# One decoder layer on one core: the second key block's attention product taken in one matmul, stages of the projection phase placed anew, and the first norm's vectors loaded through SyncE's queue

## The chip, the cores and the metric

The kernel runs on one core of one Trainium2 chip. The metric is the device time of one execution in microseconds (us). TensorE is written PE, its weight loads PEld, VectorE DVE, ScalarE ACT, GpSimd POOL and SyncE SP; SP only issues transfers and waits.

## The reference, cut to what matters

```python
proj  = x @ W_in                      # q | k | v | B | C | h | gate_attn | gate_conv
y_att = attention(q, k, v) @ W_att    # 8 heads of 64, partial rotary, causal
y_cnv = (B * causal_dwconv3(C * h)) @ W_cnv
mix   = (sigmoid(g_att) * y_att + sigmoid(g_cnv) * y_cnv) @ W_o
x     = LayerNorm(alpha * x + mix)
u     = causal_dwconv3(x @ W_up);  f = (silu(u_gate) * u_val) @ W_down
x     = LayerNorm(alpha * x + f)
```

There are 256 positions and a model width of 1024, all in float32. The block length of the attention is 256, so that with 256 positions each query attends to its own block alone: ordinary causal attention over two 128-position halves. The second half of the keys is seen by the second half of the queries only.

## The kernel before

**Products.** Every float32 product is made of three TensorE products of rounded parts: a factor is split into a high part (an ACT copy that rounds) and a low part (the DVE difference of the source and the high part), and `mm3` (lines 329 to 331) multiplies high by high, high by low and low by high. Weights come in 1 MB chunks from a packed tensor on SP's queue (line 187) into `raw`, are split on ACT (`wh`, line 211) and DVE (`wl`, line 221) half a chunk (a unit) at a time, and are used once. There are 3 `raw` buffers and 9 of `wh` and of `wl`.

**Order.** The order of all engines is written by hand. After q, k and v, PE works through numbered slots, one unit of weights and 12 matmuls of 512 columns in most: slots 0 to 11 make h, C and B, 12 to 27 the four gate blocks, 28 to 35 the two mixers' output products (`y`, in the order first and second 128 positions of the first 512 columns, then of the second 512; even slots multiply the convolution's `yT`, odd ones the attention's `aT`), 36 to 43 the product with W_o (`o`). The function `slot` first issues a slot's products, then the ACT and DVE work placed at that slot. The table `STEPS` gives each stage of the attention, the convolution and the gates a step: step 2u lies before and 2u + 1 behind the splits of slot u, and keys that end in E choose the engine (1 is DVE) of a copy. `lah` and `lal` say how many units ahead the splits run in each slot. Stages of PE (`s`, the scores, and `av`, the attention's second product) are placed by whole slots, behind the slot's own products.

**Attention.** It runs by pairs p = 0 to 3 of heads. `masked`, `exps` and `normalize` make a pair's probabilities; their 16-bit halves are turned by a transposing transfer (SP, line 476), joined again (`probs_words`), and split into high and low part in `PT` (`probs_h` on ACT, line 487; `probs_l` on DVE). `PT` is a single buffer, so that the next pair's `probs_h` waits for the matmuls of `attend`. The weights of those matmuls hold v's high and low part side by side, so one product gives both, 64 partitions each. `attend_out` copies the lower 64 partitions, `attend_sum` adds them to the upper 64, and `attend_h` and `attend_l` split the sum into `aT`.

**PSUM.** 4 banks take the accumulators of the projections; 4 more (`ps_bank`) take the scores and then the attention's products, and from slot 28 on the pairs of banks of `y`.

**Mix and first norm.** For each of the four pieces of `y` DVE makes the gated sum (`mix_conv`, `mix_att`), its 16-bit halves (`mix_halves`) are turned by a transfer on SP's queue (line 859; the third piece in two halves of 256 columns), joined (`mix_words`, lines 865 and 867) and split into `mT` (`mix_h`, line 874, and `mix_l`), which W_o's product reads. The joining and the splitting of a piece stand one behind the other: both halves of the third piece are joined before either is split. Then come the residual sum and the first norm (lines 908 to 926), PE's transposes of the first 128 positions (`x1t`, line 976) and the feed-forward part, which the change does not reach but for one store near the end.

The norm's two vectors are spread over all partitions by two transfers of 512 KB (line 902), issued by POOL into a buffer that `aT` held before:

```python
    ln1 = big.tile([P, 2, D], F32, tag="d8", name="ln1")
    for i, g in enumerate((ln1_g, ln1_b)):
        nc.gpsimd.dma_start(ln1[:, i, :], bass.AP(tensor=g.tensor, offset=g.offset, ap=[[0, P], [1, D]]))
```

Of the kernel before, what the change touches and what calls it, by code (L numbers as in the profile page):

```python
# [13 lines left out]
AF = mybir.ActivationFunctionType  # L14
ALU = mybir.AluOpType

P = 128
S = 256
# [125 lines left out]
def layer_kernel(ctx: ExitStack, tc: tile.TileContext, x, wpack, cpack, b_gate, ln1_g, ln1_b, ln2_g, ln2_b, out):  # L144
# [32 lines left out]
    def issue_dma(c):  # L177
        nonlocal xr
        while len(raws) <= c and len(raws) < len(chunks):
# [8 lines left out]
            if i == XR_CHUNK:  # L188
                xr = big.tile([P, 2, D], F32, tag="x", name="xr")
                for row in range(2):  # L190
                    nc.sync.dma_start(xr[:, row], x[0, row * P:(row + 1) * P])
# [300 lines left out]
    def attend(p):  # L492


        o = PR[p, "o"] = ps_bank(f"av{p}").rearrange("p (j s) -> p j s", j=2)
        for j in range(2):
            js = slice(j * P, (j + 1) * P)
            for a in range(2):
                nc.tensor.matmul(o[:, j], vp[:, 0, p, js], PT[:, a, j, 0:256], start=a == 0, stop=False)
            for a in range(2):  # L500
                nc.tensor.matmul(o[:, j, P:S], vp[:, 1, p, js], PT[:, a, j, 256:384], start=False, stop=a == 1)

    def attend_out(p):

        c = PR[p, "c"] = scratch([P, 2, S], f"ac{p}")
        nc.scalar.activation(c[0:HD], PR[p, "o"][HD:P], AF.Copy)

    def attend_sum(p):
        c, o = PR[p, "c"], PR[p, "o"]
        nc.vector.tensor_tensor(c[HD:P, 0], o[0:HD, 1], c[0:HD, 1], op=ALU.add)  # L510
        nc.vector.tensor_tensor(c[0:HD, 0], o[0:HD, 0], c[0:HD, 0], op=ALU.add)
# [66 lines left out]
    STEPS = {'vl': [2, 0], 'qw': [5, 6, 9, 11], 'qwE': [0, 1, 1, 0], 'qh': [7, 9, 10, 15], 'ql': [6, 8, 14, 15], 's': [5, 10], 'ml': [6, 7, 10, 10], 'm': [15, 18, 21, 27], 'e': [17, 20, 26, 32], 'n': [19, 23, 32, 38], 'w': [22, 25, 37, 43], 'wE': [0, 1, 0, 0], 'h': [23, 27, 40, 44], 'l': [24, 32, 42, 45], 'av': [13, 18, 22, 24], 'out': [27, 42, 45, 51], 'sum': [40, 43, 50, 50], 'ah': [42, 44, 52, 52], 'al': [45, 48, 52, 55], 'c1': [21, 32], 'c2a': [23, 24, 38, 39], 'c2d': [24, 29, 44, 41], 'c3': [33, 48], 'c4a': [35, 51], 'c4d': [43, 53], 'sig': 17, 'hc': [6, 8], 'zm': [15, 15], 'zh': [17, 15], 'zhE': [0, 1], 'bh': [27, 26], 'bj': [32, 33], 'bjE': [0, 1], 'c1E': [0, 0], 'lah': [5, 6, 7, 5, 5, 5, 5, 5, 4, 3, 4, 4, 4, 4, 3, 5, 5, 5, 5, 4, 4, 3, 5, 6, 7, 6, 5, 6, 6, 6, 7, 6, 6, 6, 6, 4, 2, 4, 3, 6, 7, 8, 8, 8], 'lal': [2, 5, 4, 4, 3, 3, 4, 5, 3, 3, 3, 3, 4, 3, 2, 4, 4, 4, 4, 3, 2, 2, 2, 3, 6, 6, 4, 3, 5, 5, 5, 5, 5, 5, 5, 3, 3, 4, 3, 4, 6, 6, 5, 6], 'sg': [35, 35, 46, 48, 50, 53, 61, 61], 'gb': [23, 34, 43, 50], 'gs': [31, 32, 41, 38, 48, 48, 59, 57], 'yc': [59, 63, 67, 70], 'ya': [61, 65, 69, 71], 'yaE': [0, 1, 0, 0], 'yh': [64, 66, 71, 71], 'yhE': [0, 0, 0, 1], 'yw': [68, 70, 75, 85], 'ywE': [0, 1, 0, 0], 'mh': [68, 72, 75, 85], 'mlo': [69, 73, 78, 84], 'mlw': [11, 15, 21, 22]}  # L578
# [322 lines left out]
    for i, g in enumerate((ln1_g, ln1_b)):  # L901
        nc.gpsimd.dma_start(ln1[:, i, :], bass.AP(tensor=g.tensor, offset=g.offset, ap=[[0, P], [1, D]]))
# [373 lines left out]
    for c in range(2):  # L1276
        cc = slice(c * 512, (c + 1) * 512)
        norm_apply(r0[:, cc], r0[:, cc], mv, ln2[:, 0, cc], ln2[:, 1, cc])
        for a in range(0, P, P // 2):
            nc.sync.dma_start(out[0, a:a + P // 2, cc], r0[a:a + P // 2, cc])  # L1280
# [75 lines left out]
```

## Time and profile before

| | |
|---|---|
| three timed runs | 352.75, 358.1 and 358.31 us; median 358.1 |
| profiled execution, its own time | 354.5 us |
| its span, first to last instruction | 352.4 us |
| mean granted TensorE clock in it | 0.995 |
| PE busy in the span | 344.6 us, 98% |
| DVE, ACT, POOL busy | 295.5, 253.2, 16.0 us |
| moved | 81.64 MB, 232 GB/s in the mean |

A matmul's busy time overlaps that of the next, since matmuls are pipelined; how fast PE works is read from the distance of starts. In the timeline a row has start, duration, engine, line, operation, the names of output and inputs, the shape and the count, and in brackets the idle time before it with what ended it.

### The profile page before, as it was taken

How to read it: one execution, taken by the hardware profiler on the slowest of the kernel's cores; microseconds unless marked ns; L12 is line 12 of the kernel's file. 1: busy time of each engine (PE TensorE's matmuls, PEld its weight loads, DVE VectorE, ACT ScalarE, POOL GpSimd, SP SyncE). 2: the span in 40 equal slices, each digit the busy share in tenths (PEclk: the TensorE clock that was granted, in tenths of full speed). 3: DMA queues.
4: the chain of work that ended last, by engine and by line, in shares of the span. 5: the costliest groups of instructions: out<-in, count | busy, mean ns of one | idle time of the engine just before them, and what ended most of it. 6: DMA issues, size and time to landing. Idle time of an engine off the chain costs nothing.

```text
span 352.4 us, 4621 instructions
## 1 busy us (share of the span) xinstructions
PE 344.6 (98%) x1595; PEld 286.1 (81%) x1595; DVE 295.5 (84%) x504; ACT 253.2 (72%) x386; POOL 16.0 (5%) x38
## 2 busy tenths in 40 slices
PE   9999999999999999999999999999999999999993
PEld 8888888888888888778888888888888888888883
DVE  4787769699999988799945999899799969597975
ACT  4766957799889855495566879879487878677800
POOL 2000002010000000104100000000000000000030
PEclk9999999999999999999999999999999999999998
DMA  7995968669956999985499668686887958667003
GB/s 275 426 378 223 215 188 333 95 204 272 274 170 223 340 368 218 269 293 200 74 286 313 248 163 248 218 268 184 328 227 295 307 173 267 171 262 151 0 18 102
DMA packets 56151, 81.64 MB, mean 232 GB/s; under 512 B 45632, under 2 KB 46144, under 8 KB 49088
## 3 DMA queue, kind: packets, MB, share of 16 engines
q1 hardware_dynamic: 55552, 79.25, 73.1%
q0 software_dynamic: 576, 2.10, 1.9%
q8 instruction: 12, 0.20, 0.2%
q14 instruction: 11, 0.09, 0.1%
HBM read 69.28 MB, written 1.05 MB: 200 GB/s over the span
## 4 chain that ended last, share of the span: by engine, by line
PE 86%; DVE 5%; DMA 4%; issue 2%; ACT 1%; POOL 0%; POOLq 0%; DVEq 0%; ACTq 0%
PE u L331 10%; PE u L329 10%; PE u L330 10%; PE qk L644 6%; PE d L331 5%; PE d L330 5%; PE d L329 5%; PE g L329 4%; PE g L330 4%; PE g L331 4%; DMA mixw<-mixw 4%; PE u L1117 3%; PE v L644 3%; DVE wl L221 1%; PE b L329 1%
## 5 line engine op out<-in xcount | busy, mean ns | idle before, releaser
L221 DVE TENSOR_TENSOR wl<-raw,wh 128x1024 fp32r<-128x1024 f32 x100 | 119.4, 1220 | 14.6 <-ACT wh L211 14.3
L211 ACT ACTIVATE wh<-raw 128x1024 fp32r<-128x1024 f32 x97 | 98.5, 1053 | 7.6 <-DMA raw<-in_wpack 4.5
L329 PE MATMUL u<-wh,x1T 128*128 128x512 f32 x160 | 62.3, 390 | 0.0
L331 PE MATMUL u<-wh,x1T 128*128 128x512 f32 x160 | 62.3, 389 | 0.0
L330 PE MATMUL u<-wl,x1T 128*128 128x512 f32 x160 | 62.3, 389 | 0.0
L330 PEld LDWEIGHTS u<-wl,x1T 128*128 128x128 f32 x160 | 30.0, 188 | 6.3
L331 PEld LDWEIGHTS u<-wh,x1T 128*128 128x128 f32 x160 | 30.0, 188 | 6.3
L329 PEld LDWEIGHTS u<-wh,x1T 128*128 128x128 f32 x160 | 30.0, 188 | 6.2
L244 DVE TENSOR_TENSOR wl<-raw,wh 128x1024 fp32r<-128x1024 f32 (+2 forms) x27 | 24.8, 955 | 7.7 <-ACT wh L243 7.5
L998 ACT ACTIVATE fc<-pb,consts 128x256 f32<-128x256 f32 x44 | 19.9, 500 | 15.5 <-DVE pb L1044 15.5
L331 PE MATMUL d<-wh,f 128*128 128x512 f32 x76 | 29.6, 390 | 0.0
L329 PE MATMUL d<-wh,f 128*128 128x512 f32 x76 | 29.6, 390 | 0.0
L330 PE MATMUL d<-wl,f 128*128 128x512 f32 x76 | 29.6, 389 | 0.0
L1032 ACT ACTIVATE up<-u 128x1024 uint16<-128x1024 uint16 x22 | 21.3, 1013 | 7.2 <-PE u L331 7.1
L243 ACT ACTIVATE wh<-raw 128x1024 fp32r<-128x1024 f32 (+2 forms) x27 | 21.3, 834 | 7.2 <-DMA raw<-in_wpack 7.2
L329 PE MATMUL g<-wh,xT 128*128 128x512 f32 x64 | 25.2, 393 | 0.0
L330 PE MATMUL g<-wl,xT 128*128 128x512 f32 x64 | 25.0, 390 | 0.0
L331 PE MATMUL g<-wh,xT 128*128 128x512 f32 x64 | 24.9, 389 | 0.0
L1006 DVE SCALAR_TENSOR_TENSOR fc<-pb,consts,fc 128x254 f32<-128x254 f32 x44 | 21.3, 484 | 1.6
L1004 DVE SCALAR_TENSOR_TENSOR fc<-pb,consts,fc 128x255 f32<-128x255 f32 x44 | 21.1, 480 | 0.0
L644 PE MATMUL qk<-wh,xT 128*128 128x512 f32 x60 | 19.2, 390 | 0.0
L330 PEld LDWEIGHTS d<-wl,f 128*128 128x128 f32 x76 | 14.3, 188 | 3.0
(221 smaller groups left out, 644.3 us busy)
## 6 DMA issues: line engine op xcount, KB each, us to landing
raw<-in_wpack SPq DMA_DIRECT2D x55, 1024.0 KB, 5.3
raw<-in_wpack SPq DMA_DIRECT2D x6, 896.0 KB, 11.5
gb<-in_b_gate SPq DMA_DIRECT2D x4, 256.0 KB, 5.2
xr<-in_x SPq DMA_DIRECT2D x2, 512.0 KB, 7.0
ln<-in_ln_g POOLq DMA_DIRECT2D x2, 512.0 KB, 5.1
ln<-in_ln_b POOLq DMA_DIRECT2D x2, 512.0 KB, 5.8
raw<-in_wpack SPq DMA_DIRECT2D x2, 384.0 KB, 4.4
raw<-in_wpack SPq DMA_DIRECT2D x2, 256.0 KB, 3.0
```

Of the source, the lines that this page charges most:

```text
L211: nc.scalar.activation(units[u]["h"], raw_of(u), AF.Copy)
L221: (eng or nc.vector).tensor_tensor(units[u]["l"], raw_of(u), units[u]["h"].bitcast(F32), op=ALU.subtract)
L243: nc.scalar.activation(h, src, AF.Copy)
L244: (eng or nc.vector).tensor_tensor(l, src, h.bitcast(F32), op=ALU.subtract)
L329: nc.tensor.matmul(o, ah, bh, start=start, stop=False)
L330: nc.tensor.matmul(o, ah, bl, start=False, stop=False)
L331: nc.tensor.matmul(o, al, bh, start=False, stop=stop)
L644: nc.tensor.matmul(banks[m][t], (xl if p == 2 else xh)[:, k, t * P:(t + 1) * P], wl if p == 1 else wh, start=k == 0 and p == 0, stop=k == ...
L998: nc.scalar.activation(PB["c", i][a], PB[i][:, a * S:(a + 1) * S], AF.Copy, scale=w_ffn(2, j))
L1004: nc.vector.scalar_tensor_tensor(c[:, 1:S], pb[:, a * S:a * S + S - 1], w_ffn(1, j), c[:, 1:S], op0=ALU.mult, op1=ALU.add)
L1006: nc.vector.scalar_tensor_tensor(c[:, 2:S], pb[:, a * S:a * S + S - 2], w_ffn(0, j), c[:, 2:S], op0=ALU.mult, op1=ALU.add)
L1032: nc.scalar.activation(half.rearrange("p (w n) -> p w n", w=2), PB["rows", c][t].bitcast(U16).rearrange("p (n w) -> p w n", w=2), AF.Copy)
```

## The change

1. `attend`: the two products of the second key block with the probabilities' high and low part, 128 columns each and added in one place, become one product of 256 columns into two places. Each half j of a pair gets a bank of its own, 384 columns of it used. `attend_out` becomes two copies of 256 columns, `attend_sum` gets two more sums, of 128 columns, that add the low part's place.
2. `STEPS` has other numbers in 144 of its 253 places: stages and split distances move by a few half slots, and four copies change their engine.
3. The first norm's two vectors are issued by SP in place of POOL, at the same place of the program. `xr` comes in one transfer of 1 MB in place of two, and the first half of the first output rows leaves in one store in place of two.

```diff
@@ issue_dma @@
-                for row in range(2):
-                    nc.sync.dma_start(xr[:, row], x[0, row * P:(row + 1) * P])
+                nc.sync.dma_start(xr, x[0].rearrange("(t p) d -> p t d", p=P))
@@ attend @@
-        o = PR[p, "o"] = ps_bank(f"av{p}").rearrange("p (j s) -> p j s", j=2)
+        PR[p, "o"] = []
         for j in range(2):
+            o = ps_bank(f"av{p}{j}")
+            PR[p, "o"].append(o)
             js = slice(j * P, (j + 1) * P)
             for a in range(2):
-                nc.tensor.matmul(o[:, j], vp[:, 0, p, js], PT[:, a, j, 0:256], start=a == 0, stop=False)
-            for a in range(2):
-                nc.tensor.matmul(o[:, j, P:S], vp[:, 1, p, js], PT[:, a, j, 256:384], start=False, stop=a == 1)
+                nc.tensor.matmul(o[:, 0:S], vp[:, 0, p, js], PT[:, a, j, 0:256], start=a == 0, stop=a == 1)
+            nc.tensor.matmul(o[:, P:P + S].rearrange("p (a n) -> p a n", a=2), vp[:, 1, p, js], PT[:, :, j, 256:384],
+                             start=False, stop=True, skip_group_check=True)
@@ attend_out @@
-        nc.scalar.activation(c[0:HD], PR[p, "o"][HD:P], AF.Copy)
+        for j in range(2):
+            nc.scalar.activation(c[0:HD, j], PR[p, "o"][j][HD:P, 0:S], AF.Copy)
@@ attend_sum @@
-        nc.vector.tensor_tensor(c[HD:P, 0], o[0:HD, 1], c[0:HD, 1], op=ALU.add)
-        nc.vector.tensor_tensor(c[0:HD, 0], o[0:HD, 0], c[0:HD, 0], op=ALU.add)
+        for j in range(2):
+            nc.vector.tensor_tensor(c[0:HD, j, P:S], o[j][0:HD, S:S + P], c[0:HD, j, P:S], op=ALU.add)
+        nc.vector.tensor_tensor(c[HD:P, 0], o[1][0:HD, 0:S], c[0:HD, 1], op=ALU.add)
+        nc.vector.tensor_tensor(c[0:HD, 0], o[0][0:HD, 0:S], c[0:HD, 0], op=ALU.add)
@@ the first norm's vectors @@
-        nc.gpsimd.dma_start(ln1[:, i, :], bass.AP(tensor=g.tensor, offset=g.offset, ap=[[0, P], [1, D]]))
+        nc.sync.dma_start(ln1[:, i, :], bass.AP(tensor=g.tensor, offset=g.offset, ap=[[0, P], [1, D]]))
@@ the last norm of the first rows @@
-        for a in range(0, P, P // 2):
-            nc.sync.dma_start(out[0, a:a + P // 2, cc], r0[a:a + P // 2, cc])
+        rows = P // (c + 1)
+        for a in range(0, P, rows):
+            nc.sync.dma_start(out[0, a:a + rows, cc], r0[a:a + rows, cc])
```

Of the table, the keys that matter below, by pair of heads (or by piece of the mix):

| key | stage | before | now |
|---|---|---|---|
| `av` | attention's second product (slot) | 13, 18, 22, 24 | 14, 19, 22, 23 |
| `al` | low part of `aT` | 45, 48, 52, 55 | 45, 47, 55, 55 |
| `c4d` | low part of `yT` | 43, 53 | 39, 54 |
| `qwE` | engine that joins the turned q and k | 0, 1, 1, 0 | 0, 1, 0, 0 |
| `zhE`, `bjE` | engines of two copies of the convolution | 0, 1 and 0, 1 | 1, 1 and 0, 0 |
| `yh`, `yhE` | halves of the mix | 64, 66, 71, 71; 0, 0, 0, 1 | 64, 66, 71, 74; 0, 0, 0, 0 |
| `yw` | joining of the turned mix | 68, 70, 75, 85 | 67, 71, 77, 86 |

On PE, at the third pair's attention product behind slot 22 (`av` is its bank, `vpt` holds v and `PT`, `g` is a gate block), before:

```order
L331 MATMUL g_1057<-wh_999,xT 128x512
L499 MATMUL av_1117<-vpt 128x256 x2
L501 MATMUL av_1117<-vpt 128x128 x2
L499 MATMUL av_1117<-vpt 128x256 x2
L501 MATMUL av_1117<-vpt 128x128 x2
L329 MATMUL g_1056<-wh_1028,xT 128x512
```

and now:

```order
L330 MATMUL g_1063<-wh_980,xT 128x512
L500 MATMUL av_1123<-vpt 128x256 x2
L501 MATMUL av_1123<-vpt 128x256
L500 MATMUL av_1127<-vpt 128x256 x2
L501 MATMUL av_1127<-vpt 128x256
L328 MATMUL g_1062<-wh_994,xT 128x512
```

Eight matmuls have become six, into two banks; the place is the same. The first two pairs' products stand one slot later than before, the fourth pair's one slot earlier, 12 matmuls behind the third's.

On SP, at the mix (`mixw` holds the halves, `raw` weights), before:

```order
L859 DMA_TRANSPOSE mixw<-mixw 128x8x128
L187 DMA raw_1420<-in_wpack 128x2048
L859 DMA_TRANSPOSE mixw<-mixw 128x4x128 x2
L859 DMA_TRANSPOSE mixw<-mixw 128x8x128
L187 DMA raw_1508<-in_wpack 128x2048
```

and now:

```order
L863 DMA_TRANSPOSE mixw<-mixw 128x8x128
L187 DMA raw_1405<-in_wpack 128x2048
L863 DMA_TRANSPOSE mixw<-mixw 128x4x128 x2
L906 DMA ln_1462<-in_ln_g 128x1024
L906 DMA ln_1462<-in_ln_b 128x1024
L863 DMA_TRANSPOSE mixw<-mixw 128x8x128
L187 DMA raw_1490<-in_wpack 128x2048
```

The norm's vectors stand behind the two transposes of the third piece and ahead of that of the fourth, whose halves ACT now writes and not DVE.

On DVE, ahead of the first `y` products (`ac` is the attention's sum, `ct` the convolution's result), before:

```order
L510 TENSOR_TENSOR ac_1224<-av_1181,ac_1224 64x256
L511 TENSOR_TENSOR ac_1224<-av_1181,ac_1224 64x256
L221 TENSOR_TENSOR wl_1231<-raw_1130,wh_1195 128x1024
L240 TENSOR_TENSOR aT<-ac_1136,aT 128x256
L240 TENSOR_TENSOR yT<-ct_1045,yT 128x2x256
L240 TENSOR_TENSOR aT<-ac_1224,aT 128x256
L221 TENSOR_TENSOR wl_1295<-raw_1157,wh_1267 128x1024
L221 TENSOR_TENSOR wl_1297<-raw_1157,wh_1269 128x1024
```

and now:

```order
L513 TENSOR_TENSOR ac_1227<-av_1156,ac_1227 64x128
L513 TENSOR_TENSOR ac_1227<-av_1160,ac_1227 64x128
L514 TENSOR_TENSOR ac_1227<-av_1160,ac_1227 64x256
L515 TENSOR_TENSOR ac_1227<-av_1156,ac_1227 64x256
L220 TENSOR_TENSOR wl_1261<-raw_1134,wh_1198 128x1024
L239 TENSOR_TENSOR yT<-ct_1014,yT 128x2x256
L220 TENSOR_TENSOR wl_1281<-raw_1166,wh_1237 128x1024
L220 TENSOR_TENSOR wl_1283<-raw_1166,wh_1259 128x1024
L239 TENSOR_TENSOR aT<-ac_1189,aT 128x256
L239 TENSOR_TENSOR aT<-ac_1227,aT 128x256
```

Both low parts of `aT` stand behind two more weight splits than the first of them did, and each pair's sums are four in place of two.

More of the change, by code (lines that the diff above doesn't have):

```diff
@@ L577, in layer_kernel @@
     C0 = U[OFF_H]
-    STEPS = {'vl': [2, 0], 'qw': [5, 6, 9, 11], 'qwE': [0, 1, 1, 0], 'qh': [7, 9, 10, 15], 'ql': [6, 8, 14, 15], 's': [5, 10], 'ml': [6, 7, 10, 10], 'm': [15, 18, 21, 27], 'e': [17, 20, 26, 32], 'n': [19, 23, 32, 38], 'w': [22, 25, 37, 43], 'wE': [0, 1, 0, 0], 'h': [23, 27, 40, 44], 'l': [24, 32, 42, 45], 'av': [13, 18, 22, 24], 'out': [27, 42, 45, 51], 'sum': [40, 43, 50, 50], 'ah': [42, 44, 52, 52], 'al': [45, 48, 52, 55], 'c1': [21, 32], 'c2a': [23, 24, 38, 39], 'c2d': [24, 29, 44, 41], 'c3': [33, 48], 'c4a': [35, 51], 'c4d': [43, 53], 'sig': 17, 'hc': [6, 8], 'zm': [15, 15], 'zh': [17, 15], 'zhE': [0, 1], 'bh': [27, 26], 'bj': [32, 33], 'bjE': [0, 1], 'c1E': [0, 0], 'lah': [5, 6, 7, 5, 5, 5, 5, 5, 4, 3, 4, 4, 4, 4, 3, 5, 5, 5, 5, 4, 4, 3, 5, 6, 7, 6, 5, 6, 6, 6, 7, 6, 6, 6, 6, 4, 2, 4, 3, 6, 7, 8, 8, 8], 'lal': [2, 5, 4, 4, 3, 3, 4, 5, 3, 3, 3, 3, 4, 3, 2, 4, 4, 4, 4, 3, 2, 2, 2, 3, 6, 6, 4, 3, 5, 5, 5, 5, 5, 5, 5, 3, 3, 4, 3, 4, 6, 6, 5, 6], 'sg': [35, 35, 46, 48, 50, 53, 61, 61], 'gb': [23, 34, 43, 50], 'gs': [31, 32, 41, 38, 48, 48, 59, 57], 'yc': [59, 63, 67, 70], 'ya': [61, 65, 69, 71], 'yaE': [0, 1, 0, 0], 'yh': [64, 66, 71, 71], 'yhE': [0, 0, 0, 1], 'yw': [68, 70, 75, 85], 'ywE': [0, 1, 0, 0], 'mh': [68, 72, 75, 85], 'mlo': [69, 73, 78, 84], 'mlw': [11, 15, 21, 22]}
@@ new lines, in layer_kernel @@
+    STEPS = {'vl': [0, 3], 'qw': [5, 6, 8, 10], 'qwE': [0, 1, 0, 0], 'qh': [5, 9, 8, 15], 'ql': [5, 9, 14, 16], 's': [5, 10], 'ml': [6, 7, 10, 10], 'm': [15, 18, 22, 25], 'e': [18, 20, 26, 31], 'n': [18, 22, 31, 39], 'w': [22, 26, 39, 43], 'wE': [0, 1, 0, 0], 'h': [24, 29, 40, 44], 'l': [24, 30, 42, 45], 'av': [14, 19, 22, 23], 'out': [28, 39, 48, 50], 'sum': [37, 40, 49, 50], 'ah': [43, 46, 52, 52], 'al': [45, 47, 55, 55], 'c1': [23, 31], 'c2a': [24, 25, 37, 38], 'c2d': [24, 27, 43, 43], 'c3': [36, 48], 'c4a': [38, 51], 'c4d': [39, 54], 'sig': 17, 'hc': [8, 8], 'zm': [16, 17], 'zh': [17, 18], 'zhE': [1, 1], 'bh': [27, 24], 'bj': [35, 38], 'bjE': [0, 0], 'c1E': [0, 0], 'lah': [4, 6, 7, 6, 5, 5, 4, 5, 5, 4, 6, 5, 6, 6, 6, 6, 6, 6, 5, 4, 5, 3, 5, 5, 7, 7, 7, 7, 5, 6, 7, 6, 6, 7, 7, 4, 4, 5, 2, 5, 5, 4, 5, 6], 'lal': [3, 6, 4, 4, 3, 4, 4, 4, 3, 4, 5, 4, 5, 4, 5, 5, 4, 4, 4, 3, 2, 2, 2, 3, 6, 5, 5, 6, 5, 5, 5, 5, 4, 6, 6, 3, 3, 5, 3, 3, 3, 2, 2, 2], 'sg': [36, 36, 46, 50, 51, 54, 67, 64], 'gb': [25, 37, 44, 50], 'gs': [31, 31, 41, 42, 48, 48, 58, 58], 'yc': [60, 63, 68, 70], 'ya': [62, 65, 69, 72], 'yaE': [0, 0, 0, 0], 'yh': [64, 66, 71, 74], 'yhE': [0, 0, 0, 0], 'yw': [67, 71, 77, 86], 'ywE': [0, 1, 0, 0], 'mh': [67, 73, 77, 87], 'mlo': [69, 74, 77, 88], 'mlw': [11, 15, 21, 24]}
```

## Prediction

> **What bounds the kernel now.** I read the page's shares first, then the windows by stage, then PE's timeline where a window shows PE idle.
>
> ```profile
> span 352.4 us, 4621 instructions
> ...
> PE 344.6 (98%) x1595; PEld 286.1 (81%) x1595; DVE 295.5 (84%) x504; ACT 253.2 (72%) x386; POOL 16.0 (5%) x38
> ```
>
> ```profile
> core 0: us, PE busy (x) PEld busy (x) DVE busy (x) ACT busy (x) POOL busy (x), PEclk, DMA share, GB/s
> 37.00:120.00 83.00, 83.00 (x409) 69.03 (x408) 75.19 (x146) 69.61 (x115) 3.81 (x4) 1.00 0.79 226
> 120.00:142.00 22.00, 22.00 (x99) 18.23 (x98) 18.42 (x25) 14.52 (x17) 0.00 (x0) 1.00 1.04 299
> 142.00:166.00 24.00, 22.93 (x105) 18.46 (x104) 20.63 (x29) 15.45 (x21) 3.97 (x6) 1.00 0.83 263
> 166.00:342.00 176.00, 176.00 (x778) 145.77 (x777) 149.22 (x241) 129.75 (x199) 5.63 (x7) 1.00 0.69 209
> 342.00:352.40 10.40, 4.50 (x33) 4.05 (x31) 6.36 (x17) 0.00 (x0) 0.55 (x1) 0.84 0.37 102
> ```
>
> The first number behind the stretch's length is PE. From 37 to 142 us (slots 0 to 35, all that the new table rearranges) PE has no gap, nor has it one from 166 to 342 us, which the change doesn't touch. It idles 24.00 - 22.93 = 1.07 us in W_o's product. The kernel is bound by PE, so a change of order can win no more than that hole and what PE itself is spared, but it can lose anywhere: DVE is busy 75.19 of 83 us ahead of it.
>
> The hole:
>
> ```profile
> 148.68 0.39 PE L331 MATMUL o<-wh,mT 128*128 128x512 f32 x1
> 150.04 0.50 PE L329 MATMUL o<-wh,mT 128*128 128x512 f32 x1 [0.97 <-ACT mT L874]
> 150.38 0.40 PE L330 MATMUL o<-wl,mT 128*128 128x512 f32 x1
> ```
>
> Matmuls of 512 columns start 0.23 us apart elsewhere; here 1.36 and then 0.34 us pass, so some 1.2 us are lost while PE waits for the high part of the mix's third piece. What made that late:
>
> ```profile
> 144.88 0.70 ACT L867 ACTIVATE mc<-mixw 128x512 uint16<-128x512 uint16 x1 [0.90 <-DMA mixw<-mixw]
> 149.00 0.69 ACT L867 ACTIVATE mc<-mixw 128x512 uint16<-128x512 uint16 x1 [3.41 <-DMA mixw<-mixw]
> ```
>
> ```profile
> 141.10 5.21 SPq L859 DMA_TRANSPOSE mixw<-mixw  x3
> ```
>
> ```profile
> 142.59 0.73 POOL L902 DMA_DIRECT2D ln<-in_ln_g  x1 [68.30 <-DVE mc L865]
> 143.32 0.53 POOL L902 DMA_DIRECT2D ln<-in_ln_b  x1
> ```
>
> ```profile
> DMA to landing us min/median/max: 3.7/5.9/6.5
> DMA to landing us min/median/max: 4.1/5.4/6.8
> ```
>
> (The landing rows are those of `mixw` and of `ln`.) The first half of the piece lands 3.7 us after its issue at 141.10. The second, issued 1.2 us later and of the same size, takes 6.5. Between them POOL issues the norm's 1 MB, under way from 142.6 until 150 or so.
>
> **The change part by part.** The sum starts at the profiled execution's own 354.5 us.
>
> *The attention's products on PE.* One pair before:
>
> ```profile
> 104.86 0.40 PE L499 MATMUL av<-vpt 128*128 128x256 f32 x2
> 105.09 0.34 PE L501 MATMUL av<-vpt 128*128 128x128 f32 x2
> 105.26 0.45 PE L499 MATMUL av<-vpt 128*128 128x256 f32 x2
> 105.55 0.34 PE L501 MATMUL av<-vpt 128*128 128x128 f32 x2
> 105.73 0.45 PE L329 MATMUL g<-wh,xT 128*128 128x512 f32 x1
> 106.01 0.40 PE L330 MATMUL g<-wl,xT 128*128 128x512 f32 x1
> ```
>
> By starts, two matmuls of 128 columns take 105.26 - 105.09 = 0.17 us, two of 256 take 0.23 or 0.29, so 0.115 to 0.145 each. Where 0.17 us become one matmul of 256 columns, 0.025 to 0.055 us are saved, eight times: 0.2 to 0.45 us. The other end: a pair with the step back to 512 columns takes 106.01 - 104.86 - 0.23 = 0.92 us; six matmuls at half the 0.23 us of 512 columns would take 0.69, which saves 0.23 four times, 0.9 us. The new matmul writes two places in steps of 128 columns, which no row shows; I take 0.4, from the rows of the same shape: **-0.4 us** (0.2 to 0.9). The Trainium skill (TensorE: Matmul & The Clock Gate, Back-to-back issue gap) speaks against even that: it gives an isolated matmul of 128 columns 134 cycles and one of 256 columns 262, so that by it a pair of the first costs 268 and the exchange saves 6 cycles, 0.02 us in eight. The rows have the short ones at 0.085 us, well above its 0.056; by the skill the sum would be 0.4 us longer.
>
> *The norm's vectors on SP's queue.* Behind the third piece's second transpose, at 141.1 + 2 x 1.2 = 143.5 us, SP now issues them, and only then the fourth piece's transpose. The last reader of `aT`, on which the buffer waits, starts at 141.9 us (below), so SP doesn't wait there. The second transpose no longer has a megabyte of another queue beside it; if it takes the 3.7 us of the first half, it lands at 142.4 + 3.7 = 146.1 in place of 149.0. The next limit is ACT. The fourth piece's halves are now written there, ahead of the joining: DVE ends the fourth sum near 145, the copy takes 1.06 (as the mix's other copy of that size), a weight split 1.05, and the two joins of 0.70 end near 148.5, the first split of `mT` 0.4 later: 148.9. PE wants it at 148.68 + 0.23 - 0.4 (its own gain) = 148.5. So 0.4 of the 1.2 us stays: **-0.8 us** (bounds: -1.2, all of it gone, and 0: were the landing unchanged, the copy and the split would still fit into ACT's 3.41 us of idle time ahead of 149.00, so a loss is excluded). Queued behind the vectors are the fourth piece's transpose and the next weights. At the 6.8 us of the slowest `ln` row the vectors land at 150.3, the transpose (median 5.9) by 156; its product is wanted only when PE has done the first rows, near 159, and the norm reads the vectors first there too. That move is covered by 3 us.
>
> *The transposes of x1.* PE's eight small transposes wait a little for the norm:
>
> ```profile
> PEld x1t L976 <- DVE x L914: 0.3, 1, 0.3
> 155.82 0.68 DVE L924 SCALAR_TENSOR_TENSOR xr<-xr,o 128x512 f32<-128x512 f32 x1
> ```
>
> (waits, then DVE's timeline). The residual sum at 155.82 follows four weight splits with no idle time, which themselves followed the late `mT`; now three stand there, one having gone ahead. With `mT` earlier the residual follows PE instead: **-0.3 us** (0 to 0.3).
>
> *The new places from slot 0 to 35.* Nothing can be won here, PE being full. Work added to DVE is eight sums of 128 columns, priced at the nearest row:
>
> ```profile
> L371 DVE TENSOR_TENSOR ra<-ra,rb 128x128 f32<-128x128 f32 x2 | 0.6, 293 | 0.1
> L392 ACT ACTIVATE qw<-qkHT 128x1024 uint16<-128x1024 uint16 x2 | 2.3, 1174 | 0.7 <-DMA qkHT<-qkH 0.7
> L390 DVE COPY qw<-qkHT 128x1024 uint16<-128x1024 uint16 x2 | 1.5, 754 | 0.0
> L506 ACT ACTIVATE ac<-av 64x512 f32<-64x512 f32 x4 | 2.3, 587 | 0.0
> ```
>
> so 8 x 0.29 = 2.3 us. Three copies go from DVE to ACT and one comes back, a net two: 2 x 0.75 = 1.5 us off DVE, 2 x 1.17 = 2.3 on ACT. ACT's four evacuations become eight of half the length, each between 0.29 and 0.59: 0 to 2.4 us more. DVE's load grows by 0.8, ACT's by up to 4.7. The windows have 7.8 us idle on DVE and 13.4 on ACT up to 120 us, which cover this in the sum. Where it lands is another matter, at two places:
>
> ```profile
> 105.88 0.85 ACT L487 ACTIVATE vpt<-sm 128x768 fp32r<-128x768 f32 x1 [1.56 <-PE av L501]
> 106.76 0.96 DVE L240 TENSOR_TENSOR vpt<-sm,vpt 128x768 fp32r<-128x768 f32 x1
> ```
>
> The fourth pair's `PT` can be written only when the third's products are over, and ends at 107.72. Its products now come 12 x 0.227 = 2.7 us behind the third's, near 108.4 less the 0.3 gained by then. That leaves 0.4 us if both engines are free at once; before it was 3.7.
>
> ```profile
> 116.76 0.42 DVE L510 TENSOR_TENSOR ac<-av,ac 64x256 f32<-64x256 f32 x1
> 118.41 1.21 DVE L221 TENSOR_TENSOR wl<-raw,wh 128x1024 fp32r<-128x1024 f32 x1
> 119.54 0.41 DVE L240 TENSOR_TENSOR aT<-ac,aT 128x256 fp32r<-128x256 f32 x1
> 119.88 0.67 DVE L240 TENSOR_TENSOR yT<-ct,yT 128x512 fp32r<-128x512 f32 x1
> L331 PE MATMUL y<-wh,aT x16: 388/390/390, 123.5 to 141.9; 128*128 128x512 f32 x16
> ```
>
> (the last is from the tile's own view). From the sums at 116.76 in the new order: four of 0.29 and four of 0.43 to 119.6, a split of 1.13 to 120.8, `yT` to 121.4, two splits to 123.6, the third pair's `aT` to 124.1. PE's first low product of `aT` starts at 123.5; the third pair's comes six matmuls later, at 124.9, less 0.4 gained: 124.5. That leaves 0.4 us. Two covers of 0.4 us, in a stretch where an engine can easily be a little later than the sum: I take **+0.2 us** (0 to 2.5; the upper end is all of DVE's 2.3 us on PE's path).
>
> *The rest.* `xr` in one transfer spares SP one issue near 120 us; it is first read at 155.82. One store fewer in the end stands among transfers that leave while PE still multiplies. Both at nothing.
>
> The sum: 354.5 - 0.4 - 0.8 - 0.3 + 0.2 = **353.2 us**. The three runs shown lie from 352.75 to 358.31 with the median at 358.1: the profiled execution is near their lower end, and the same 1.3 us off the median would be 356.8. The spread of the runs, not the change, sets most of the range.
>
> **The rivals.**
>
> *The hole stays.* The second transpose is late for another reason than the norm's vectors, or ACT's new copy takes what the transfer gives. For it: ACT is only 0.4 us from being the limit by my own sum. Against it: two transfers of one size, one queue and neighbouring issues differ by 2.8 us exactly while the vectors move. The second and third terms fall away: 354.5 - 0.4 + 0.2 = 354.3 us. A sentence of the Trainium skill (Trainium Kernel Development and Optimization, Key Constraints) is on this side: transfers of SP, ACT and POOL run on the same 16 engines and interleave, and issuing from several saves issue time only. By it the vectors would burden the piece from either queue; that they now start behind it in its own queue is what my term rests on.
>
> *Slower: PE waits for the low part of `aT`.* Its place is the odd slots of `y`, near 124 us. Everything that DVE is late there beyond 0.4 us is PE's, and nothing behind gives it back, since PE is full from 166 us on. For it: two more splits and four more sums in front, DVE at 91% from 37 to 120. Against it: DVE idles 7.8 us in that stretch, so part of the sums is absorbed earlier. It outweighs the 1.5 us of gains once DVE is 1.9 us late; with the whole 2.3 of the new sums and as much again of waits on ACT's longer work (4.6 - 0.4 = 4.2 on PE) the time is 354.5 - 1.5 + 4.2 = 357.2 us.
>
> **How the numbers follow.** The forecast gets 0.6, the hole that stays 0.22, the late `aT` 0.15; 0.03 is for what I don't see. The forecast's own range on the profiled execution's footing is 352.0 to 354.0. The range to 8 in 10 takes in the late `aT` (357.2), and runs that fall where two of the three fell, 358.1 less little; below, the lowest run less the largest gain, 352.75 - 2.2 = 350.6. So 350.6 to 358.2. About 2% is what a measurement of this kernel can tell from no change. Faster by 2% than the median means under 350.9, which only runs at the low end with the full gain reach: 0.07. Slower by 2% is 7.2 us, far beyond the late `aT`: 0.04. Within: 0.89.
>
> **What would show it.** Right: attention pairs near 0.8 us by starts; the third piece's second transpose landing within 4.5 us of its issue, with no idle of more than 0.5 us in front of `o`; no PE gap near 108 and 124 us; 166 to 342 us as before. Wrong: the second join of the third piece still near 149 us; PE idle released by `vpt` or `aT`; DVE waiting for ACT between 100 and 120 us.

## The result and the profile after

The changed kernel takes 352.23 us (median of 14 runs, 351.62 to 352.65). The kernel before, in as many runs beside it, has a median of 354.88 us (352.49 to 359.62). The ratio is 0.9949, with a 95% interval of 0.9929 to 0.9968: half a per cent faster, inside the 2% that count as no change and clear of the noise. Runs more than 1.5% above the fastest of their kernel are left out of the ratio, which is why it lies nearer to 1 than the two medians do, and of the table of experiments below, where therefore no range can exceed 5.3 us.

The profiled execution took 352.56 us (354.5 before). Its page begins:

```profile
span 350.6 us, 4607 instructions
...
PE 343.9 (98%) x1587; PEld 286.3 (82%) x1587; DVE 295.9 (84%) x510; ACT 255.0 (73%) x392; POOL 14.1 (4%) x36
```

The windows by stage (the first number behind the length is PE's busy time):

```profile
core 0: us, PE busy (x) PEld busy (x) DVE busy (x) ACT busy (x) POOL busy (x), PEclk, DMA share, GB/s
37.00:120.00 83.00, 83.00 (x404) 68.80 (x404) 75.24 (x151) 70.22 (x118) 3.06 (x4) 1.00 0.76 222
120.00:142.00 22.00, 22.00 (x99) 18.21 (x98) 19.94 (x27) 16.59 (x21) 0.00 (x0) 1.00 0.94 313
142.00:166.00 24.00, 24.00 (x111) 19.97 (x110) 21.12 (x31) 17.01 (x23) 4.49 (x4) 1.00 0.75 252
```

The 1.07 us of idle PE between 142 and 166 us are gone. The added sums and copies show as 0.05 us more of DVE and 0.6 of ACT up to 120 us, and 1.5 and 2.1 us more from there to 142; PE has no gap in either stretch.

PE's timeline at the first of the four attention products:

```profile
81.91 0.40 PE L500 MATMUL av<-vpt 128*128 128x256 f32 x2
82.14 0.28 PE L501 MATMUL av<-vpt 128*128 128x256 f32 x1
82.27 0.40 PE L500 MATMUL av<-vpt 128*128 128x256 f32 x2
82.50 0.28 PE L501 MATMUL av<-vpt 128*128 128x256 f32 x1
82.62 0.40 PE L328 MATMUL g<-wh,xT 128*128 128x512 f32 x1
82.86 0.40 PE L329 MATMUL g<-wl,xT 128*128 128x512 f32 x1
```

By starts, a pair with the step back to 512 columns now takes 82.86 - 81.91 - 0.23 = 0.72 us, where it took 0.92.

SP's queue and ACT at the third piece of the mix:

```profile
140.78 2.50 SPq L863 DMA_TRANSPOSE mixw<-mixw  x2
143.34 0.57 SPq L906 DMA_DIRECT2D ln<-in_ln_g  x1
143.96 0.42 SPq L906 DMA_DIRECT2D ln<-in_ln_b  x1
145.95 1.24 SPq L863 DMA_TRANSPOSE mixw<-mixw  x1
```

```profile
144.87 1.06 ACT L862 ACTIVATE mixw<-mc 128x1024 uint16<-128x1024 uint16 x1 [0.66 <-DVE mc L853]
145.83 1.04 ACT L210 ACTIVATE wh<-raw 128x1024 fp32r<-128x1024 f32 x1
146.78 1.26 ACT L871 ACTIVATE mc<-mixw 128x512 uint16<-128x512 uint16 x2
147.94 0.71 ACT L878 ACTIVATE mT<-mc 128x256 fp32r<-128x256 f32 x2
```

The second half of the piece, the later of the two transposes in SP's first row, lands 2.4 us after its issue, at 144.5. Both halves (`x2` in the third of ACT's rows) are joined at 146.78 with no bracket behind them: ACT no longer waits for the transposes, and its own order is the limit. The joins end at 148.0 and the first split of `mT` at 148.3, early enough for PE, which comes to it at 148.8. The residual sum, which followed late weight splits before, now follows PE:

```profile
153.75 0.69 DVE L928 SCALAR_TENSOR_TENSOR xr<-xr,o 128x512 f32<-128x512 f32 x1 [0.62 <-PE o L330]
```

Where the time went, by the first starts on PE: to the first slot (`h`), from there to the first `y`, to the first `o`, to the first transpose of x1, to the first product of the feed-forward part (`u`), to PE's end, to the span's end.

| profiled kernel | to h | h to y | y to o | o to x1t | x1t to u | u to end | tail |
|---|---|---|---|---|---|---|---|
| before | 37.26 | 83.09 | 21.76 | 20.32 | 3.96 | 180.12 | 5.85 |
| after | 37.97 | 82.27 | 21.76 | 19.04 | 3.62 | 180.06 | 5.89 |
| difference | +0.71 | -0.82 | 0 | -1.28 | -0.34 | -0.06 | +0.04 |

The +0.71 at the start isn't the change's: the same changed kernel, profiled once more (below), reached `h` at 37.16.

### The profile page after: what moved, and what is told of

Read it like the earlier page. It is cut to its first block, busy times and chain, and to the rows that moved or that the text cites. A ratio compares the mean times of both kernels' runs of the same rounds, so it can differ in the third digit from the quotient of the medians.

```text
span 350.6 us, 4607 instructions
## 1 busy us (share of the span) xinstructions
PE 343.9 (98%) x1587; PEld 286.3 (82%) x1587; DVE 295.9 (84%) x510; ACT 255.0 (73%) x392; POOL 14.1 (4%) x36
## 3 DMA queue, kind: packets, MB, share of 16 engines
q0 software_dynamic: 288, 1.05, 0.8%
HBM read 69.28 MB, written 1.05 MB: 201 GB/s over the span
## 4 chain that ended last, share of the span: by engine, by line
PE 95%; issue 2%; DVE 1%; POOLq 0%; POOL 0%; DVEq 0%
PE u L329 10%; PE u L328 10%; PE u L330 10%; PE qk L648 6%; PE d L329 5%; PE d L328 5%; PE d L330 5%; PE g L328 4%; PE g L330 4%; PE g L329 4%; PE v L648 3%; PE u L1121 3%; PE o L330 2%; PE o L328 2%; PE y L330 2%; PE y L328 2%
## 5 line engine op out<-in xcount | busy, mean ns | idle before, releaser
L328 PEld LDWEIGHTS d<-wh,f 128*128 128x128 f32 x76 | 14.3, 188 | 3.0
```

The lines of the kernel that those rows point to most:

```text
L328: nc.tensor.matmul(o, ah, bh, start=start, stop=False)
```

## The experiments

The kernel before, timed beside each set of four, had 353.61 us (352.59 to 357.75), 353.41 (352.51 to 357.24) and 353.49 (352.61 to 357.60). The changed kernel was timed in one of the sets alone, so a difference to it from another set is uncertain by the 0.2 us between these medians at least. Stretches are of the one profiled execution, as in the table above.

| kernel | median us | range us | h to y | y to o | o to x1t | tail |
|---|---|---|---|---|---|---|
| changed, again | 352.25 | 351.69 to 352.69 | 82.27 | 21.76 | 19.05 | 5.83 |
| changed, old products | 352.95 | 352.52 to 353.92 | 83.09 | 21.76 | 19.05 | 5.83 |
| changed, old places | 353.07 | 352.15 to 354.16 | 82.46 | 22.06 | 19.04 | 5.83 |
| changed, vectors on POOL | 352.91 | 352.04 to 356.42 | 82.27 | 21.76 | 19.04 | 5.96 |
| the same, held back | 352.48 | 351.95 to 355.77 | 82.27 | 21.76 | 19.04 | 5.98 |
| changed, vectors on ACT | 354.44 | 353.34 to 358.20 | 82.27 | 21.76 | 20.87 | 5.84 |
| changed, two transfers more | 352.51 | 351.93 to 353.05 | 82.27 | 21.76 | 19.04 | 6.38 |
| before, new products | 353.83 | 352.86 to 356.80 | 83.42 | 22.08 | 19.04 | 5.89 |
| before, vectors on SP | 354.37 | 353.70 to 355.04 | 83.09 | 21.76 | 19.05 | 6.94 |
| the same, x in one | 353.93 | 353.51 to 354.68 | 83.09 | 21.76 | 19.04 | 6.79 |
| the same, one store fewer | 353.90 | 353.46 to 354.60 | 83.09 | 21.76 | 19.04 | 6.64 |
| the same, both | 353.00 | 352.51 to 353.67 | 83.09 | 21.76 | 19.04 | 5.85 |

### The products

The changed kernel once more, to stand beside the others:

> The changed kernel once more, as the measure for those timed beside it: median near 352.2 us, all times within 1.5 us of each other, no idle stretch of PE over 0.4 us between the first slot and the last product.

It took 352.25 us, as expected. Beside it, `attend`, `attend_out` and `attend_sum` as before, in the new places:

```diff
-            nc.tensor.matmul(o[:, P:P + S].rearrange("p (a n) -> p a n", a=2), vp[:, 1, p, js], PT[:, :, j, 256:384],
-                             start=False, stop=True, skip_group_check=True)
+            for a in range(2):
+                nc.tensor.matmul(o[:, j, P:S], vp[:, 1, p, js], PT[:, a, j, 256:384], start=False, stop=a == 1)
...
```

> The changed kernel with the attention's products, evacuations and sums of the kernel before. My theory: four pairs cost 0.2 us more of PE each, from the first slot to the first product of y 83.1 us in place of 82.3, and the time is 0.7 to 0.9 us over the changed kernel. Rival (the saving of the products is partly eaten by the sums and copies that came with them): 0.2 to 0.5 us over it.

It took 352.95 us, 0.70 more, as in my theory if at its lower end, and the stretch from `h` to `y` is 83.09 in place of 82.27 us. In the new places the products bring PE 0.82 us and the time 0.7.

### The places

The kernel before with the new products, evacuations and sums alone, in the old places, the vectors on POOL:

```diff
+            nc.tensor.matmul(o[:, P:P + S].rearrange("p (a n) -> p a n", a=2), vp[:, 1, p, js], PT[:, :, j, 256:384],
+                             start=False, stop=True, skip_group_check=True)
...
```

> The kernel before with the attention's product, its evacuation and its sums of the change, at the old places, the vectors still on GpSimd's queue. My theory: a pair takes 0.72 us of PE in place of 0.92 by starts, four pairs 0.8 us less, and the added sums and copies are covered in the old places too; the hole in the product with W_o stays: 0.6 to 0.9 us under the kernel before. Rival (the sums and copies that came with it need the new table): gaps on PE released by vpt or aT between 100 and 130 us, and a time at or above the kernel before.

It took 353.83 us, no less than the kernel before (ratio 0.9998, 0.9965 to 1.0031). My theory fell, and the rival was right that a gap comes, though not by `vpt` or `aT`. PE's timeline at the first `y`:

```profile
119.89 0.39 PE L331 MATMUL g<-wh,xT 128*128 128x512 f32 x1
121.27 0.47 PE L329 MATMUL y<-wh,yT 128*128 128x512 f32 x1 [0.99 <-DVE ac L516]
```

PE waits for the last of the attention's sums. From slot 28 on `y` takes the banks that the attention's products held, and these come free with the last sum that reads them; the third and the fourth pair now hold two banks each and have four sums each. The hole of the kernel before isn't in this profile (19.04 us from `o` to x1t), although the vectors are on POOL's queue. The second half is late here too, and ACT waits for it:

```profile
148.47 0.69 ACT L872 ACTIVATE mc<-mixw 128x512 uint16<-128x512 uint16 x1 [2.05 <-DMA mixw<-mixw]
```

But PE, held up at `y`, starts `o` 1.2 us later than in the kernel before (143.34 against 142.11), so that it no longer has to wait. Part of what PE lost at `y` it would otherwise have lost at the hole.

The second way to the same place is the changed kernel with the old table:

```diff
-    STEPS = {'vl': [0, 3], 'qw': [5, 6, 8, 10], 'qwE': [0, 1, 0, 0],
...
+    STEPS = {'vl': [2, 0], 'qw': [5, 6, 9, 11], 'qwE': [0, 1, 1, 0],
...
```

> The changed kernel with the table of places of the kernel before. My theory: the new places are worth nothing where PE is full, and the vectors' move alone closes the hole: within 0.3 us of the changed kernel. Rival one (the old places leave PE waiting for aT or PT now that the products are faster): gaps between 100 and 130 us and 0.5 to 2 us over the changed kernel. Rival two (the table closes half of the hole): an idle stretch of 0.3 us or more ahead of the third piece's products stays and the time is 0.4 to 0.8 us over the changed kernel.

It took 353.07 us, 0.8 over the changed kernel: the first rival, with the wait at another place than it names. Its DVE and PE:

```profile
119.59 0.42 DVE L515 TENSOR_TENSOR ac<-av,ac 64x256 f32<-64x256 f32 x1
119.93 1.21 DVE L220 TENSOR_TENSOR wl<-raw,wh 128x1024 fp32r<-128x1024 f32 x1
```

```profile
119.74 0.39 PE L330 MATMUL g<-wh,xT 128*128 128x512 f32 x1
120.15 0.47 PE L328 MATMUL y<-wh,yT 128*128 128x512 f32 x1
```

The last sum ends at 120.01, `y` starts 0.14 us later, and 0.41 instead of 0.23 us behind the product ahead of it. Behind it `yT` is late as well; from `h` to `o` the kernel needs 0.49 us more than the changed one. In the changed kernel, DVE's timeline has the last sum of the same line at

```profile
119.03 0.42 DVE L515 TENSOR_TENSOR ac<-av,ac 64x256 f32<-64x256 f32 x1
119.37 1.21 DVE L220 TENSOR_TENSOR wl<-raw,wh 128x1024 fp32r<-128x1024 f32 x1
```

ending at 119.45, and `y` starts on time at 120.23. Measured from `h`, DVE reaches the sums there 0.84 us earlier than with the old table; ahead of that place the new table has taken two copies of 0.75 us off DVE and put one of 0.69 on it. So the new places win nothing of their own (the changed kernel with the old products, at 352.95, equals the kernel before with vectors, x and store of the change, at 353.00), but without them the products' 0.7 us is lost again.

### The queue of the vectors

The changed kernel with the vectors on POOL again:

```diff
-        nc.sync.dma_start(ln1[:, i, :], bass.AP(tensor=g.tensor, offset=g.offset, ap=[[0, P], [1, D]]))
+        nc.gpsimd.dma_start(ln1[:, i, :], bass.AP(tensor=g.tensor, offset=g.offset, ap=[[0, P], [1, D]]))
```

> The changed kernel with the two vectors issued by GpSimd again, all else as changed. My theory: the second transpose of the third piece lands 6 us or more after its issue, PE's hole of 1 us or more comes back ahead of the third piece's products: 1.0 to 1.6 us over the changed kernel. Rival (the new table's other places of the mix's stages closed the hole, the queue has no part in it): within 0.3 us of the changed kernel and no hole.

The median is 352.91 us, 0.66 over the changed kernel, and the runs reach from 352.04 to 356.42. The two ratios to the kernel before overlap (0.9950 to 1.0017 here, 0.9935 to 0.9977 for the changed kernel again), so it is the range of 4.4 us against 1.0, more than the median, that speaks for the theory. The profiled execution, one of the faster ones at 352.44 us, has no hole, but no late half either: the second half lands 2.4 us after its issue, and both are there when ACT comes to join them. It shows neither the theory nor the rival. What goes with a late half can be read across the four profiles whose vectors are on another queue and not held back, from the traces:

| profile | second half's issue ahead of the vectors' | lands after its issue | behind the first half |
|---|---|---|---|
| changed, vectors on POOL | 0.71 us | 2.4 us | 0.6 us |
| before, new products | 0.51 | 5.1 | 2.7 |
| before | 0.20 | 6.5 | 4.1 |
| changed, vectors on ACT (below) | -0.32 | 6.8 | 3.0 |

In all ten other profiles the vectors are issued 1.2 us or more behind the second half, and it lands 0.4 to 0.6 us behind the first. So a few tenths of a microsecond between two queues go with 2 to 4 us at the landing. Next, a copy of two 16-bit words by POOL that reads the last word of the first and the first of the second turned half, ahead of POOL's transfers:

```diff
+    nc.gpsimd.tensor_copy(ln1[:, 0, 0:1].bitcast(U16), mixw[:, 0, 1535:1537])
-        nc.sync.dma_start(ln1[:, i, :], bass.AP(tensor=g.tensor, offset=g.offset, ap=[[0, P], [1, D]]))
+        nc.gpsimd.dma_start(ln1[:, i, :], bass.AP(tensor=g.tensor, offset=g.offset, ap=[[0, P], [1, D]]))
```

> The changed kernel with the vectors on GpSimd's queue again, but ahead of them a copy of two 16-bit words by GpSimd that reads both turned halves of the mix's third piece, so that the vectors can't start before that piece has landed. My theory (with the vectors on GpSimd's queue what costs time, and what spreads the times by 4 us and more from run to run, is that they move while the third piece is on its way): within 0.3 us of the changed kernel, and times within 1.5 us of each other. Rival (it is GpSimd's queue as such, whenever it is used there): the median 0.5 us or more over the changed kernel, and times spread over 3 us or more. A third outcome: the fourth piece's transposing transfer is now the one that meets the vectors, lands after 152 us, and PE waits for it ahead of 159 us.

The median is 352.48 us, 0.23 over the changed kernel, and eleven of twelve runs lie between 351.95 and 353.32 us, one at 355.77. POOL's queue as such costs next to nothing, then. The vectors now meet the fourth piece, whose transpose is issued 0.17 us behind the first of them and lands 6.6 us later (4.1 in the changed kernel), and ACT waits for it:

```profile
151.77 1.19 ACT L871 ACTIVATE mc<-mixw 128x1024 uint16<-128x1024 uint16 x1 [1.06 <-DMA mixw<-mixw]
```

In this execution PE doesn't wait (19.04 us from `o` to x1t), against the third outcome.

And the vectors on a queue beside the transposes, without POOL:

```diff
-        nc.sync.dma_start(ln1[:, i, :], bass.AP(tensor=g.tensor, offset=g.offset, ap=[[0, P], [1, D]]))
+        nc.scalar.dma_start(ln1[:, i, :], bass.AP(tensor=g.tensor, offset=g.offset, ap=[[0, P], [1, D]]))
```

> The changed kernel with the vectors issued by ScalarE, so that they move on another queue beside the third piece's transposes, as with GpSimd, but without GpSimd. My theory (traffic on a second queue beside the transposes): the second transpose lands 5 us or more after its issue in some executions, times spread over 2 us or more, and the median is 0.3 to 1 us over the changed kernel, part of which is the two issues that ScalarE now makes ahead of the third piece's join. Rival (GpSimd's queue alone does it): within 0.3 us of the changed kernel and within 1.5 us of each other.

The median is 354.44 us, 2.2 over the changed kernel and more than I expected, over a range of 4.9 us. In the profiled execution the second half of the third piece is late again, and PE has a hole of 1.90 - 0.23 = 1.7 us; ACT's timeline, then PE's:

```profile
146.65 0.67 ACT L871 ACTIVATE mc<-mixw 128x512 uint16<-128x512 uint16 x1
148.81 0.69 ACT L871 ACTIVATE mc<-mixw 128x512 uint16<-128x512 uint16 x1 [1.49 <-DMA mixw<-mixw]
```

```profile
147.96 0.39 PE L330 MATMUL o<-wh,mT 128*128 128x512 f32 x1
149.86 0.50 PE L328 MATMUL o<-wh,mT 128*128 128x512 f32 x1 [1.50 <-ACT mT L878]
```

ACT's own two issues don't make it: counted from `h` they bring ACT to the first half 0.5 us later than in the changed kernel, and then it waits another 1.49 us for the second. Nor do the new places close the hole once the half is late, which was the rival of the first experiment here. One thing in this profile isn't the vectors': the second piece's transpose, issued more than 7 us ahead of them, lands after 8.4 us (5.9 in the changed kernel), and the first half of the third piece after 5.0 (3.1). But the second half lands another 3.0 us behind the first. So it is the megabyte beside the piece, from either queue. The ranges say the same. The kernels whose vectors stand behind the third piece in SP's own queue (the changed one and eight of the twelve here, 109 runs) have ranges of 1.0 to 2.0 us, those with the vectors on another queue (the kernel before and four here) of 3.8 to 5.2, where the kernel that holds them back owes its 3.8 to a single run.

### The number of SP's transfers

The first experiment was the vectors' move alone, in the kernel before:

```diff
-        nc.gpsimd.dma_start(ln1[:, i, :], bass.AP(tensor=g.tensor, offset=g.offset, ap=[[0, P], [1, D]]))
+        nc.sync.dma_start(ln1[:, i, :], bass.AP(tensor=g.tensor, offset=g.offset, ap=[[0, P], [1, D]]))
```

> The kernel before with one line changed: the first norm's two vectors are issued by SyncE and not by GpSimd. My theory (the vectors' traffic beside the mix's third piece holds the piece's second transposing transfer): that transfer lands within 4.5 us of its issue, PE's idle stretch of 1.2 us ahead of the third piece's products goes nearly whole, and the wait ahead of the x1 transposes with it: 1.2 to 1.6 us under the kernel before. Rival (the second transpose is late for a reason of its own, its place in the queue): the hole and the time stay, within 0.3 us. A side question: if the vectors on GpSimd's queue are also what spreads the times of the kernel before over some 7 us, this kernel's times lie within 1.5 us.

The hole went (19.05 us from `o` to x1t), the second half landed 2.7 us after its issue and the range fell to 1.3 us. But in place of the gain of 1.2 to 1.6 us that I expected, the median was 354.37 us, no better than the kernel before (ratio 1.0008, 0.9983 to 1.0032). The profile has the loss in the tail: 6.94 us from PE's end, not 5.85. The stretch around the last stores, in 40 slices of 0.063 us (busy share of the DMA engines in tenths, then what they moved), and further down in the same view the code queue's packets and a large store's time to landing:

```profile
DMA  1000038999999999999998510000000000000000
GB/s 33 0 0 0 0 147 319 344 369 451 393 344 344 320 393 369 393 393 369 393 369 295 197 25 0 25 25 25 25 25 25 25 25 0 0 0 0 0 0 0
...
q14 instruction: 1, 0.01, 0.8%
...
out<-res SPq DMA_DIRECT2D x1, 192.0 KB, 2.5
```

Behind the bulk, from slice 24 on, about half a microsecond of 25 GB/s: single packets of 1536 bytes, one after the other, as if one DMA engine were late. The view's list of queues has one packet of another kind in this stretch, of code, and the trace has it at 349.07 us, 8 KB long, in the middle of the stores. In the kernel before it comes at 350.96, when they are over. SP issues two transfers more here than before. The change as a whole doesn't: it also takes one off x and one off the stores. So both of these, then each alone:

```diff
-                for row in range(2):
-                    nc.sync.dma_start(xr[:, row], x[0, row * P:(row + 1) * P])
+                nc.sync.dma_start(xr, x[0].rearrange("(t p) d -> p t d", p=P))
...
-        for a in range(0, P, P // 2):
-            nc.sync.dma_start(out[0, a:a + P // 2, cc], r0[a:a + P // 2, cc])
+        rows = P // (c + 1)
+        for a in range(0, P, rows):
+            nc.sync.dma_start(out[0, a:a + rows, cc], r0[a:a + rows, cc])
```

> The kernel before with the vectors on SyncE's queue and, as in the change, x in one transfer and one store fewer at the end: SyncE issues as many transfers as in the kernel before, where the kernel with the vectors alone moved issued two more. In that one the stretch from PE's end to the end of the span was 6.95 us and not 5.85, an 8 KB packet of the code-loading queue standing among the last stores. My theory (two more instructions on SyncE bring a load of its code forward among the last stores): the stretch is 5.7 to 6.0 us again, and the time 0.8 to 1.2 us under that of the vectors alone, near 353.2 us. Rival (that stretch was chance): no difference over 0.3 us in the medians.

> The kernel before with the vectors on SyncE's queue and x in one transfer; the stores as before. The vectors alone took 354.4 us, with 6.95 us from PE's end to the end of the span; with x in one transfer and one store fewer 353.0 and 5.85 us. If it is the number of SyncE's instructions that decides (a load of its code among the last stores): here one more than in the kernel before, so the end lies between, or flips to one of the two. If it is the stores: as with the vectors alone, 354.2 to 354.5 us and a late end.

> The kernel before with the vectors on SyncE's queue and one store fewer at the end; x in two transfers. If the number of SyncE's instructions decides: the same as with x in one transfer and the stores as before. If it is the stores: the early end, 5.8 to 6.0 us behind PE, and 352.9 to 353.2 us.

Both together give 353.00 us and a tail of 5.85, in which the same view ends with the bulk:

```profile
GB/s 393 344 311 197 66 74 246 393 393 393 295 319 344 393 394 394 369 393 369 393 393 369 271 99 131 0 0 0 0 0 0 0 0 0 0 0 0 0 0 0
```

Each alone gives 353.93 and 353.90 us, tails of 6.79 and 6.64, and the packet of code between the second and the third store. It doesn't matter which transfer is saved, only how many: with two more than before the tail is 6.94, with one more about 6.7, with none 5.85. That speaks for the number of SP's transfers and against the stores themselves. SP's own issues of the three stores change with it, here in the kernel before and then with the vectors on SP:

```profile
348.44 1.39 SPq L1314 DMA_DIRECT2D out<-res  x3
```

```profile
347.20 1.60 SPq L1314 DMA_DIRECT2D out<-res  x3
```

They take 1.60, 1.63 and 1.64 us in the three kernels with a late end and 1.39 in all others. The extra quarter of a microsecond lies between the first and the second store with two transfers more and between the second and the third with one, 1.2 to 1.5 us ahead of the packet. The same two edits undone in the changed kernel, the diff above the other way round:

> The changed kernel with x in two transfers and the output's first half in two stores again, so that SyncE issues two transfers more than in either kernel. My theory (a load of SyncE's code falls among the last stores): the stretch from PE's end to the end of the span grows from 5.9 us to 6.7 to 7.0, and the time by 0.8 to 1.2 us. Rival (the two edits are worth nothing, as I predicted): within 0.3 us of the changed kernel.

The median is 352.51 us, 0.26 over the changed kernel, and the tail 6.38 us. The median is not clear of the rival (ratio to the kernel before 0.9943 to 0.9988, the changed kernel's 0.9935 to 0.9977); the tail, in one profile, is between the two. Here the packet comes at 348.96 us, with the stores just over, and SP issues them in 1.39 us, so the load hardly touches them. What holds the end up is in the traces, in SP's last instructions. SP's transfers report their landings to eight semaphores (counters), taken in turn, and at the end of its program SP waits for these eight in a fixed order, 0.06 us for each that has nothing left to wait for. With as many transfers as in the kernel before, the last store has the semaphore that comes last, and the span ends 0.90 to 0.92 us behind its landing. With two more it has the one that comes first, so that seven waits follow, and the span ends 1.26 and 1.31 us behind it; with one more it has that of the second wait (1.19 and 1.20 us), and with two fewer, the vectors on POOL, that of the sixth (1.05 us in both kernels). That is 0.3 to 0.4 us of each late end, and most of the 0.5 in the changed kernel. The rest, in the kernel before, is the extra time at SP's issues and a last store that lands 2.2 to 2.5 us after its issue in place of 1.9 to 2.0, where the load lies among the stores. That the load is what delays them is argued from its place; the gap in SP's issues points to SP's own code. Why the same number of transfers puts it at another place in the changed kernel stays open.

## Why the prediction was right, and where it was not

The class and the range held, and the mechanisms named for the first three terms are the ones that the profile shows. The sum, 353.2 us, was 1.0 us above the median. Most of that is its start: 354.5 us was one execution's time, while the kernel before has medians of 353.4 to 353.6 beside the experiments. That from there the fall is 1.2 us (353.49 to 352.25), so near the 1.3 of the forecast, is luck. The vectors with x and the store brought 0.4 (353.41 to 353.00) where the second and third term together say 1.1, and the products in the new places 0.75 (353.00 to 352.25) where the first and fourth say 0.2. Between the two profiled executions, with the large hole in one of them, the steps add up to 2.5 us. The steps in turn:

- **The attention's products, -0.4 us.** Mis-sized: -0.82 us of PE, 0.70 of the time. I priced the new product from the two rows of its own shape (0.025 to 0.055 us each) and put the pitch of 0.115 us for all matmuls of a pair at the far end. The exchange itself gave what I took, 0.05 us (0.17 to 0.12) eight times; the other half comes from the neighbours, so the far end was right: the step behind the short matmuls fell from 0.29 to 0.23 us, and the step back to 512 columns from 0.28 to 0.24. By the isolated figures of the Trainium skill (TensorE: Matmul & The Clock Gate, Back-to-back issue gap) it would be 0.02 us in all, and the measured 0.2 us for each pair decides against using them here; the same section says itself that they count too little for short matmuls in a stream of weight loads and matmuls, and has about 81 ns at 128 columns there, near the 85 of the prediction's rows.
- **The vectors' queue, -0.8 us.** Right in kind, too small for the profiled execution: all of the 1.28 us went. The 0.4 us that I left for ACT did not come up. ACT does set the join (146.78, no wait), but it ends with the split of the first half at 148.3, and PE asks for it at 148.8. For the median it is less, since, as it seems, that execution's hole was larger than most: undoing this edit alone costs 0.66 us by medians of two sets, not clear of none, and the kernel before with this edit, x and store gains 0.4 us on the median of the kernel before (ratio 0.9986, 0.9964 to 1.0009, which by itself is not clear of none).
- **The transposes of x1, -0.3 us.** Right: 3.96 to 3.62 us.
- **The new places, +0.2 us.** Neither cover of 0.4 us gave way, so 0 and not +0.2. But "nothing can be won here, PE being full" was asked of the wrong kernel. With the new products and the old places PE is not full: `y` waits for the banks that the attention's sums hold, and from `h` to `o` 0.5 us are lost in one profile (104.52 against 104.03) and 1.5 in the other (105.50). I had followed `PT` and `aT`, the data, and not the banks. The new places cost nothing because they pay for that wait. One of the three copies that I took off DVE, that of the fourth piece's halves, lies at 144.4 us, behind both covers: ahead of them DVE was spared one copy, not two.
- **x and the store, "both at nothing".** Wrong in the same way: against the kernel before they are nothing only because the vectors added two transfers to SP and these take two away. Left out, they cost 1.4 us in the old kernel and 0.26 here, the latter not clear of none but with a tail longer by 0.5 us in the profile.
- **The rivals.** The hole that stays fell: the vectors did hold the piece up, and ACT's new copy didn't take the gain. The rule of the Trainium skill that I set beside it (Trainium Kernel Development and Optimization, Key Constraints: transfers from several engines interleave, and issuing from several saves issue time only) covers half of it. They do interleave, and for that very reason the queue is not free to choose: 352.25 us behind the transposes in one queue, 354.44 beside them in another. The late `aT` didn't come.

The step that failed outright is one of the range: "The spread of the runs, not the change, sets most of the range." The spread was the change's business. The kernel before runs from 352.5 to over 357 us, and every kernel whose vectors meet a transpose on another queue has a range of 3.8 us or more; in the changed kernel they start 1.3 us behind the second half, and its runs lie within 1.0 us. I had a hole that came from a race between two queues on one side and a wide spread on the other, and did not ask whether the one makes the other. That the runs near 357 us lose their time at this very place is argued from which kernels have them, and from the table of four profiles, where a few tenths between the issues go with 2 to 4 us at the landing; no profile here is of such a run, and the largest hole in one is the 1.7 us above.

## What to carry to other kernels

A wait on a small transfer that shares the DMA engines with a large one on another queue can come out differently in each run: a wide spread of times beside such a wait in the profile was its sign here, and putting the large one behind the small one in the same queue ended both. When a product is made cheaper by more sums elsewhere, follow the banks it holds to their next user as well as the data. Price an edit against the kernel that it will stand in: three of the parts here gain little or nothing alone, and the sum of them gains 1.3 us.

## What the runs showed of the hardware that was not expected

- Short matmuls slow the ones behind them: two of 256 columns take 0.29 us by starts behind two of 128, and 0.23 behind one of 256; the first step at 512 columns takes 0.28 and 0.24.
- A small transposing transfer is fragile: the second half piece lands 0.4 to 0.6 us behind the first when 1 MB on another queue is issued 0.7 us or more behind it, and 2.7 to 4.1 us behind it when that megabyte is issued 0.5 us behind it or earlier (5.1 to 6.8 us after its own issue).
- The number of SP's transfers alone sets 0.3 to 0.4 us at the end of these kernels: it decides which of the eight semaphores that SP waits for at the end, one behind the other, is the last store's. In the kernel before, one or two transfers more also bring a code load of 8 KB in among the last stores, and it ends 0.8 to 1.1 us later behind PE's end.
- Two executions of the same kernel reached the first slot at 37.97 and 37.16 us: 0.8 us of difference between profiles says nothing about an edit unless the stretches are compared one by one.
